# A sheet carried between column strips: four writes cut another way, and one read in place of four

## The chip, the cores and the metric

One core of a Trainium2 chip runs the whole kernel. The metric is the time of one execution in microseconds (us), measured on the device; less is better. The engines are TensorE (PE, with its weight loads PEld apart), VectorE (DVE), ScalarE (ACT), GpSimd (POOL) and SyncE (SP). SP does no arithmetic: it issues DMA transfers, one after another in the order of the program, and stands still where one of them has to wait.

## The reference: what is computed

Two layers of an encoder over 256 tokens of width 2048. Each layer projects the normed input to three groups of heads, works on them, and projects back:

```python
for l in range(DEPTH):                      # DEPTH = 2
    h = rmsnorm(x, norm_g[l])
    proj = h @ w_in[l]                      # 2048 x 7168
    a_x, a_b, a_c, a_g, d_q, d_k, d_v, d_g, m_q, m_g = jnp.split(proj, offsets, axis=-1)
    y_a = short_gated_conv(a_x, a_b, a_c, conv_w[l], conv_b[l]) * jax.nn.silu(a_g)
    # y_d: differential attention, 6 heads, on normed d_q, d_k; gated by silu(d_g)
    # y_m: attention into 256 memory tokens, 4 heads, keys and values from mem @ w_mem_kv[l]
    y = jnp.concatenate([y_a, y_d, y_m], axis=-1) @ w_out[l]
    x = x + y
```

All of it is float32. The two large products, with `w_in` and with `w_out`, are most of the work.

## The kernel before, in words

**The products.** Weights stream from DRAM in tiles of 512 KB (`raw`, 128 partitions x 2 x 512 float32, four buffers; some come as two halves of 256 KB). ACT rounds each to its leading part (`hi`, line 297), DVE makes the rest (`lo`, line 298), and PE multiplies the tokens' two parts (`xT`, `yT`) with them in three passes (line 308): 12 matmuls for a tile. `hi` and `lo` have `PARTS // CK` = 4 buffers each. A few pairs of row tiles go through a scheme with seven products in place of eight (`seven`, line 354; its weights are called `xq` and `wide`). A scheduler sets the order of what isn't pinned; lines with `keep_in_program_order` (often as `pin`) stay as they are written.

**The side work** runs beside the products as generators. `tasks` and `side` hold them, and each `yield n` gives back control for n weight tiles.

**The carry.** The heads need their data with tokens and channels exchanged. DVE's transpose exchanges within blocks of 32 x 32, so what remains is to move blocks: a sheet has 128 partitions = four column strips `a` of 32 partitions, each with four pieces `b` of `r` floats, and piece b of strip a has to go to strip b, as its piece a. `carry(sheet, to)` does that through a DRAM tile `d`, whose order is (b, c, a, r), with c the partition within a strip: four writes (line 492), then `yield 2`, then four reads. All of them are issued by SP and pinned. SP's queue is also that of all weights, so a weight tile that stands behind a read in the program waits until that read is issued, and the read waits until the writes have landed.

Where the target has three dimensions (`len(to.shape) == 3`), strip by strip as it lies in `d`, the reads are those of line 497; where its pieces are laid down in another order (in `pair` and in `turn_sheet(ordered=True)`) they are those of line 499, in runs of 32 floats.

Those who call it: `turn_sheet` (queries and keys `sh`, the memory queries `mqT`, the gates `bgT`), `pair` and `mem_pair` (attention weights `sh`, and the heads' results `yn`), the gate of the memory heads, and `conv` (its input `sh`). In all it is 32 carries of four writes each: 22 with writes of 128 KB, 8 with writes of 64 KB, 2 with writes of 192 KB.

`strips_by_rows` (line 778) is another function and is not changed: POOL issues it to load the first layer's `x` as strips, 32 transfers of 64 KB, `st[:, n] <- src[...].rearrange("p (b r) -> b p r", b=NA)`: 128 partitions in the SBUF, and in DRAM 4 strips of 32 rows of 128 floats.

Of the kernel before, what the change touches and what calls it, by code (L numbers as in the profile page):

```python
# [36 lines left out]
B = 32  # L37
NA = P // B
# [13 lines left out]
def encoder(ctx: ExitStack, tc: tile.TileContext, x, mem, norm_g, w_in, conv_w, conv_b,  # L52
            dq_g, dk_g, lq1, lk1, lq2, lk2, head_g, mem_norm_g, w_mem_kv, mq_g, mk_g, w_out, out):
    nc = tc.nc
# [19 lines left out]
    def nm(s):  # L74
        uid[0] += 1
        return f"{s}_{uid[0]}"
# [391 lines left out]
    def turn_sheet(src, dst=None, of=None, wait=5, ordered=False):  # L468


        if of is None:
            tc.keep_in_program_order(nc.vector.transpose(src, src))
        else:
            for t in range(NT):
                tc.keep_in_program_order(nc.vector.transpose(
                    src[:, :, :, t], of[:, t].rearrange("p (j b c) -> p b j c", b=NA, c=B)))
        flat = src.rearrange("p b j t i -> p b (j t i)")
        if ordered:
            yield wait
            yield from carry(flat, dst.rearrange("p j (t a i) -> p (j t) a i", t=NT, a=NA))  # L480
            return dst
        to = src.rearrange("p b j t i -> p (b j t i)") if dst is None else dst.rearrange("p j r -> p (j r)")
        yield wait
        yield from carry(flat, to.rearrange("p (a r) -> p a r", a=NA))
        return moved(to)

    def carry(sheet, to):


        d = dram.tile([NA, B, NA, sheet.shape[-1]], F32, name=nm("d"))  # L490
        for a in range(NA):
            tc.keep_in_program_order(nc.sync.dma_start(d[:, :, a].rearrange("b c r -> c b r"), sheet[a * B:(a + 1) * B]))
        yield 2
        of = d.rearrange("b c a (n i) -> (b c) a n i", i=B)
        for a in range(NA):
            if len(to.shape) == 3:
                tc.keep_in_program_order(nc.sync.dma_start(to[:, a], d.rearrange("b c a r -> (b c) a r")[:, a]))
            else:
                tc.keep_in_program_order(nc.sync.dma_start(to[:, :, a], of[:, a]))

    def silu2(dst, src, st, t):

# [53 lines left out]
    def pair(heads, begin, end, v):  # L556
# [18 lines left out]
        yield 4  # L575
        flat = sh.rearrange("p b h n c -> p (b h n c)")
        yield from carry(sh.rearrange("p b h n c -> p b (h n c)"), flat.rearrange("p (n a i) -> p n a i", a=NA, i=B))
        eT = flat.rearrange("p (h t k q) -> p h t k q", h=2, t=NT, k=NT)
        while held["yn"] == 2 or held["closed"]:
# [891 lines left out]
```

## Time and profile before

| | us |
|---|---|
| median of 3 runs | 910.44 (910.21 to 910.46) |
| the profiled execution | 910.81 |
| its span in the profile | 909.0 |
| PE busy | 903.3 (99%) |
| DVE busy | 744.6 (82%) |
| ACT busy | 584.5 (64%) |
| DMA queue q1 (SP's), share of the 16 DMA engines' time | 72.1% |

The profile is of one execution. "Busy" is time in which an engine worked on an instruction; the granted TensorE clock is full in all 40 slices of the span. The DMA rows give the transfers by their tiles (`out<-in`), how many there were, the KB of one, and the median time from issue to landing. `SPq` is SP's queue of issues.

### The profile page before, as it was taken

To read this page: it belongs to the slowest core of one execution; us is meant where nothing else is said; L and a number is where in the kernel's file an instruction comes from. 1 tells how busy PE (TensorE), PEld (TensorE's weight loads), DVE (VectorE), ACT (ScalarE), POOL (GpSimd) and SP (SyncE) were. 2 spreads that over 40 slices of the span, in tenths; PEclk is the share of its full clock that TensorE was granted. 3 is DMA by queue.
4 is the path that set the end of the run, shared out by engine and by line. 5 is a ranking of instruction groups with operands and counts; after the bars stand their busy time and mean duration, and the time that the engine had idled before them with its cause. 6 is when DMAs were issued, how large, how long until landed. Compare 5 with 4: busy or idle time off the path is not lost.

```text
span 909.0 us, 12804 instructions
## 1 busy us (share of the span) xinstructions
PE 903.3 (99%) x4161; PEld 744.6 (82%) x4161; DVE 744.6 (82%) x1073; ACT 584.5 (64%) x1135; POOL 135.5 (15%) x197
## 2 busy tenths in 40 slices
PE   9999999999999999999999999999999999999998
PEld 6887888888888888888888888888888888888887
DVE  5558889889888698998799768877987799898896
ACT  6668867757676666655566656676676676655452
POOL 2377241200030101000020202220031101000000
PEclk9999999999999999999999999999999999999999
DMA  8899876678657987879767982878478967988842
GB/s 293 281 260 266 269 269 203 214 255 275 165 187 221 297 247 232 273 251 323 261 197 237 277 276 83 279 255 277 135 235 234 273 219 257 283 272 303 273 157 92
DMA packets 164467, 219.38 MB, mean 241 GB/s; under 512 B 38568, under 2 KB 89576, under 8 KB 164400
## 3 DMA queue, kind: packets, MB, share of 16 engines
q1 hardware_dynamic: 158752, 210.81, 72.1%
q0 software_dynamic: 4448, 6.69, 2.8%
q10 hardware_dynamic: 1200, 1.07, 0.3%
q8 instruction: 32, 0.52, 0.3%
q14 instruction: 35, 0.29, 0.1%
HBM read 197.49 MB, written 21.00 MB: 240 GB/s over the span
## 4 chain that ended last, share of the span: by engine, by line
PE 96%; ACT 2%; DMA 1%; issue 1%; DVE 0%; ACTq 0%
PE acc L308 80%; PE x L354 6%; PE acc L354 5%; PE s L608 1%; PE po L516 1%; DMA raw<-in_w_mem_kv_dram 1%; PE po L745 1%; ACT hi L916 0%; ACT sq L823 0%; PE pt L761 0%; DVE lo L917 0%; ACT xf L795 0%; DMA va<-in_mem_norm_g_dram 0%; PE acc L934 0%; ACT xT L797 0%
## 5 line engine op out<-in xcount | busy, mean ns | idle before, releaser
L308 PE MATMUL acc<-hi,xT 128*128 128x512 f32 x1536 | 482.4, 391 | 0.0
L298 DVE TENSOR_TENSOR lo<-raw,hi 128x1024 fp32r<-128x1024 f32 x238 | 288.3, 1219 | 77.9 <-ACT hi L297 72.7
L297 ACT CAST hi<-raw 128x1024 fp32r<-128x1024 f32 x238 | 248.0, 1050 | 161.9 <-PE acc L308 104.0
L308 PEld LDWEIGHTS acc<-hi,xT 128*128 128x128 f32 x1536 | 288.0, 188 | 60.3 <-ACT hi L297 0.3
L308 PE MATMUL acc<-lo,xT 128*128 128x512 f32 x768 | 299.5, 390 | 0.0
L308 PEld LDWEIGHTS acc<-lo,xT 128*128 128x128 f32 x768 | 144.2, 188 | 29.4
L308 PE MATMUL acc<-hi,yT 128*128 128x512 f32 (+1 forms) x432 | 134.7, 388 | 0.0
L308 PEld LDWEIGHTS acc<-hi,yT 128*128 128x128 f32 x432 | 81.0, 188 | 16.8
L308 PE MATMUL acc<-lo,yT 128*128 128x512 f32 x216 | 83.5, 388 | 0.0
L308 PE MATMUL acc<-hi,memT 128*128 128x512 f32 x248 | 78.6, 393 | 0.0
L381 ACT CAST hi<-xq 128x1024 fp32r<-128x1024 f32 x42 | 44.0, 1049 | 34.7 <-DVE xq L384 19.8
L917 DVE SCALAR_TENSOR_TENSOR lo<-raw,cva,hi 128x1024 fp32r<-128x1024 f32 (+1 forms) x34 | 40.8, 1217 | 22.5 <-ACT hi L916 22.4
L381 DVE TENSOR_TENSOR lo<-xq,hi 128x1024 fp32r<-128x1024 f32 x42 | 51.3, 1222 | 4.7 <-ACT hi L381 4.5
L308 PEld LDWEIGHTS acc<-hi,memT 128*128 128x128 f32 x248 | 46.1, 188 | 9.6 <-ACT hi L916 0.3
L308 PE MATMUL acc<-lo,memT 128*128 128x512 f32 x124 | 48.7, 392 | 0.4 <-DVE lo L917 0.2
L308 PEld LDWEIGHTS acc<-lo,yT 128*128 128x128 f32 x216 | 40.6, 188 | 8.4
L916 ACT ACTIVATE hi<-raw,cva 128x1024 fp32r<-128x1024 f32 (+1 forms) x34 | 36.5, 1098 | 6.9 <-DMA raw<-in_w_mem_kv_dram 6.7
L443 POOL TENSOR_SCALAR ss<-ss,st 128x8 f32<-128x8 f32 (+1 forms) x16 | 12.2, 764 | 179.4 <-ACT sq L440 179.3
L381 ACT CAST hi<-wide 128x1024 fp32r<-128x1024 f32 x21 | 21.8, 1047 | 25.9 <-DVE wide L384 11.3
L354 PE MATMUL x<-hi,yT 128*128 128x512 f32 x96 | 35.4, 390 | 0.0
L192 POOL TENSOR_TENSOR rs<-ss,root 128x8 f32<-128x8 f32 (+1 forms) x20 | 33.4, 1669 | 1.6
L381 DVE TENSOR_TENSOR lo<-wide,hi 128x1024 fp32r<-128x1024 f32 x21 | 25.5, 1221 | 6.1 <-ACT hi L381 6.0
(232 smaller groups left out, 1132.9 us busy)
## 6 DMA issues: line engine op xcount, KB each, us to landing
raw<-in_w_in_dram SPq DMA_DIRECT2D x162, 512.0 KB, 4.7
raw<-in_w_out_dram SPq DMA_DIRECT2D x54, 512.0 KB, 5.1
raw<-in_w_mem_kv_dram SPq DMA_DIRECT2D x30, 512.0 KB, 5.8
raw<-in_w_in_dram SPq DMA_DIRECT2D x60, 256.0 KB, 4.1
xq<-in_w_in_dram SPq DMA_DIRECT2D x52, 256.0 KB, 5.2
d<-sh SPq DMA_DIRECT2D x88, 128.0 KB, 4.5
sh<-d SPq DMA_DIRECT2D x80, 128.0 KB, 4.1
wide<-in_w_out_dram SPq DMA_DIRECT2D x10, 512.0 KB, 6.5
```

Of the source, the lines that this page charges most:

```text
L192: nc.gpsimd.tensor_tensor(r, t, root[:, 0:n], ALU.pow)
L297: nc.scalar.copy(hi, raw)
L298: nc.vector.tensor_tensor(lo_, raw, hi.bitcast(F32), ALU.subtract)
L308: i = nc.tensor.matmul(acc, left, right, start=start, stop=stop)
L354: nc.tensor.matmul(acc, left[a], right[b], start=first and i == 0, stop=last and i == 2)
L381: return ((hi, pin(nc.scalar.copy(hi, src))), (lo, pin(nc.vector.tensor_tensor(lo, src, hi.bitcast(F32), ALU.subtract))))
L443: nc.gpsimd.tensor_scalar(ss[:, t], ss[:, t], 1.0 / gs, col(st, ET, t), ALU.mult, ALU.add)
L516: nc.tensor.matmul(po[:, t, :], eT[:, i, t, k, :], v[:, k, h * P:(h + 1) * P], start=k == 0, stop=k == NT - 1)
L608: pin(nc.tensor.matmul(s[c][:, i, :], yT[rows, a, h, i * P:(i + 1) * P], yT[rows, b, CG + h, :], start=n == 0, stop=n == 2))
L745: nc.tensor.matmul(po, left, right, start=at == 0, stop=at == 3 * NT - 1)
L916: both = (nc.scalar.activation(hi[:, j], raw[:, j], AF.Copy, scale=g), nc.vector.scalar_tensor_tensor(lo[:, j], raw[:, j], g, hi[:, j].bit ...
L917: nc.vector.scalar_tensor_tensor(lo[:, j], raw[:, j], g, hi[:, j].bitcast(F32), ALU.mult, ALU.subtract))
```

## The change

The same four pieces of four strips pass through the same DRAM tile, at the same places in it. What differs is how they are cut into transfers. A write took one strip of 32 partitions with its four pieces, so its two sides were both 32 x 4 x r. Now it takes one piece of all 128 partitions: the SBUF side is 128 x r, and the DRAM side, `d[b].rearrange("c a r -> a c r")`, is 4 x 32 x r. And where the target has three dimensions, one read of 128 partitions x 4r comes in place of four of 128 x r. The reads of line 499 stay.

```diff
         d = dram.tile([NA, B, NA, sheet.shape[-1]], F32, name=nm("d"))
-        for a in range(NA):
-            tc.keep_in_program_order(nc.sync.dma_start(d[:, :, a].rearrange("b c r -> c b r"), sheet[a * B:(a + 1) * B]))
+        for b in range(NA):
+            tc.keep_in_program_order(nc.sync.dma_start(d[b].rearrange("c a r -> a c r"), sheet[:, b]))
         yield 2
+        if len(to.shape) == 3:
+            tc.keep_in_program_order(nc.sync.dma_start(to, d.rearrange("b c a r -> (b c) a r")))
+            return
         of = d.rearrange("b c a (n i) -> (b c) a n i", i=B)
         for a in range(NA):
-            if len(to.shape) == 3:
-                tc.keep_in_program_order(nc.sync.dma_start(to[:, a], d.rearrange("b c a r -> (b c) a r")[:, a]))
-            else:
-                tc.keep_in_program_order(nc.sync.dma_start(to[:, :, a], of[:, a]))
+            tc.keep_in_program_order(nc.sync.dma_start(to[:, :, a], of[:, a]))
```

The order on PE, DVE, ACT and POOL stays as it was; on SP the same transfers stand at the same places, with other shapes. The first place is SP's queue in the first layer, around the memory queries (`mqT`), a pair's attention weights (`sh`) and a pair's results (`yn`), at 279 to 297 us of the profile. The size in a row is that of the side that is written. Before:

```order
L492 DMA d_2978<-sh_2703 32x4x256 x4
L492 DMA d_2983<-sh_2781 32x4x256 x4
L294 DMA raw_2990<-in_w_in_dram 128x2x256 x2
L492 DMA d_3009<-yn_2592 32x4x128 x4
L294 DMA raw_3014<-in_w_in_dram 128x2x256 x2
L497 DMA mqT_2267<-d_2978 128x256 x4
L499 DMA sh_2781<-d_2983 128x8x32 x4
L294 DMA raw_3061<-in_w_in_dram 128x2x256 x2
L497 DMA yn_2592<-d_3009 128x128 x4
```

and with the change:

```order
L492 DMA d_2969<-sh_2694 4x32x256 x4
L492 DMA d_2974<-sh_2772 4x32x256 x4
L294 DMA raw_2981<-in_w_in_dram 128x2x256 x2
L492 DMA d_3000<-yn_2583 4x32x128 x4
L294 DMA raw_3005<-in_w_in_dram 128x2x256 x2
L495 DMA mqT_2258<-d_2969 128x1024
L499 DMA sh_2772<-d_2974 128x8x32 x4
L294 DMA raw_3049<-in_w_in_dram 128x2x256 x2
L495 DMA yn_2583<-d_3000 128x512
```

Nothing changed places: the writes of line 492 have 4 as their outermost count where they had 32, and two groups of four reads are one read each. The second place is SP's queue in the first layer around the gates (`bgT`), a pair's results and a memory pair's attention weights, at 368 to 389 us. Before:

```order
L492 DMA d_3893<-sh_2742 32x4x384 x4
L294 DMA raw_3905<-in_w_in_dram 128x2x512
L294 DMA raw_3925<-in_w_in_dram 128x2x512
L492 DMA d_3943<-yn_3506 32x4x128 x4
L497 DMA bgT_3743<-d_3893 128x384 x4
L294 DMA raw_3960<-in_w_in_dram 128x2x256 x2
L294 DMA raw_3988<-in_w_in_dram 128x2x256 x2
L497 DMA yn_3506<-d_3943 128x128 x4
L492 DMA d_3979<-sh_3794 32x4x256 x4
L294 DMA raw_4024<-in_w_in_dram 128x2x256 x2
L497 DMA sh_3794<-d_3979 128x256 x4
```

and with the change:

```order
L492 DMA d_3869<-sh_2733 4x32x384 x4
L294 DMA raw_3881<-in_w_in_dram 128x2x512
L294 DMA raw_3901<-in_w_in_dram 128x2x512
L492 DMA d_3919<-yn_3488 4x32x128 x4
L495 DMA bgT_3719<-d_3869 128x1536
L294 DMA raw_3933<-in_w_in_dram 128x2x256 x2
L294 DMA raw_3961<-in_w_in_dram 128x2x256 x2
L495 DMA yn_3488<-d_3919 128x512
L492 DMA d_3952<-sh_3770 4x32x256 x4
L294 DMA raw_3994<-in_w_in_dram 128x2x256 x2
L495 DMA sh_3770<-d_3952 128x1024
```

Here too the places are the same; the six weight loads (`raw`) between the first write and the last read have three reads before them or among them where there were twelve.

## The prediction

> **What bounds the kernel now.** First the page's first part and the busy time by stage, the stage being that from the first carry to the last:
>
> ```profile
> PE 903.3 (99%) x4161; PEld 744.6 (82%) x4161; DVE 744.6 (82%) x1073; ACT 584.5 (64%) x1135; POOL 135.5 (15%) x197
> ...
> 150.00:835.00 685.00, 685.00 (x3195) 567.11 (x3194) 578.43 (x857) 447.11 (x887) 73.46 (x104) 1.00 0.77 244
> ```
>
> The second row's columns are the stage, its length, then busy us and count of PE, PEld, DVE, ACT and POOL, the granted clock, the DMA share and GB/s. PE is busy in 685.00 of 685.00 us. TensorE is the bound, and in the stage of the carries there is no wait of it that a faster carry could shorten. So the change can win next to nothing; the question is whether it costs. Then the DMA side, the queue of SP and the carries' transfers:
>
> ```profile
> q1 hardware_dynamic: 158752, 210.81, 72.1%
> ...
> d<-sh SPq DMA_DIRECT2D x88, 128.0 KB, 4.5
> sh<-d SPq DMA_DIRECT2D x80, 128.0 KB, 4.1
> ```
>
> The first row gives packets, MB and the share of 16 DMA engines' time. It gives the rate of one DMA engine while it works: 210.81 MB / (0.721 x 16 x 909.0 us) = 20.1 bytes per ns. A write of 128 KB needs 131072 / 20.1 = 6.52 us of one engine's time: 0.41 us if 16 share it. Of its 4.5 us to landing the rest is latency and what stands ahead of it. Last, who waits in SP's queue:
>
> ```profile
> SPq L497 <- DMA d<-sh: 15.1, 16, 2.8
> ...
> 368.34 2.99 SPq L492 DMA_DIRECT2D d<-sh  x4
> 371.82 1.06 SPq L294 DMA_DIRECT2D raw<-in_w_in_dram  x2
> 372.98 2.06 SPq L492 DMA_DIRECT2D d<-yn  x4
> 375.28 3.64 SPq L497 DMA_DIRECT2D bgT<-d  x4
> 379.02 2.18 SPq L294 DMA_DIRECT2D raw<-in_w_in_dram  x4
> ```
>
> In 16 places the read already waits for the writes to land (15.1 us in all, 2.8 at most), and weights (`raw`) are queued right behind it. Whatever makes a write land later holds up weights.
>
> **Step 1: over how many DMA engines a write is spread.** All writes of before have 32 as the outermost count of both sides. Those of after have 128 in the SBUF and 4 in DRAM. No SP transfer of before has such sides, but POOL's loads of `x` (line 778) do, the other way round: 4 x 32 rows in DRAM, 128 partitions in the SBUF. Their stage, 46 to 82 us:
>
> ```profile
> DMA packets 4413, 8.92 MB, mean 248 GB/s; under 512 B 2127, under 2 KB 2127, under 8 KB 4409
> ...
> raw<-in_w_mem_kv_dram SPq DMA_DIRECT2D x11, 512.0 KB, 5.8
> xt<-in_x_dram POOLq DMA_DIRECT2D x32, 64.0 KB, 5.7
> xq<-in_x_dram SPq DMA_DIRECT2D x1, 512.0 KB, 8.6
> kd<-sh POOLq DMA_DIRECT2D x3, 128.0 KB, 4.8
> ```
>
> 64 KB with these sides take 5.7 us, 128 KB of the same queue with the old sides (`kd<-sh`, 32 x 4 x 256) 4.8. And the small packets: all rows of these transfers are 512 B or longer, so a packet under 512 B carries no data. Suppose that each transfer leaves one on each of 16 engines: 47 transfers make 752, but there are 2127. The 1375 too many are 43 for each `xt` load. That is near 48 = 12 x 4, as if 12 of 16 engines had only empty pieces to do, four each, and 4 engines carried all. It is an inference, but I take from it that such a transfer runs on four DMA engines, and SP's writes as well. The ends are a cost of 0 (16 engines, as every SP transfer has now) and that of four.
>
> [...]
>
> On four engines a write of 128 KB takes 6.52 / 4 = 1.63 us of each in place of 0.41. A carry of four such writes puts 4 x 1.22 = 4.9 us more on each of the four; of 64 KB 2.4 us, of 192 KB 7.3 us. In all 22 x 4.9 + 8 x 2.4 + 2 x 7.3 = 142 us. Every weight tile needs all 16 engines, so it lands when the last of the four is done.
>
> **Step 2: what of it the four engines have room for.** DMA share by stage, cut around the carries; columns as above:
>
> ```profile
> 278.00:307.00 29.00, 29.00 (x150) 24.02 (x149) 21.13 (x42) 19.78 (x40) 0.83 (x4) 1.00 0.87 250
> 307.00:340.00 33.00, 33.00 (x156) 27.57 (x155) 27.29 (x42) 21.91 (x46) 3.58 (x6) 1.00 0.90 275
> 344.00:357.00 13.00, 13.00 (x67) 11.02 (x66) 12.23 (x21) 8.35 (x20) 2.18 (x3) 1.00 0.81 252
> 366.00:396.00 30.00, 30.00 (x139) 24.94 (x139) 27.35 (x40) 18.02 (x26) 0.00 (x0) 1.00 0.93 295
> 404.00:428.00 24.00, 24.00 (x113) 20.09 (x112) 19.43 (x31) 11.82 (x17) 0.00 (x0) 1.00 0.95 320
> 686.00:714.00 28.00, 28.00 (x143) 22.87 (x142) 18.96 (x39) 17.54 (x41) 4.19 (x10) 1.00 0.92 264
> 714.00:745.00 31.00, 31.00 (x148) 25.88 (x147) 26.57 (x42) 20.79 (x43) 1.21 (x3) 1.00 0.88 271
> 749.00:763.00 14.00, 14.00 (x74) 11.93 (x74) 13.86 (x23) 9.88 (x22) 1.63 (x3) 1.00 0.91 293
> 771.00:801.00 30.00, 30.00 (x140) 24.94 (x140) 26.90 (x40) 17.66 (x26) 0.00 (x0) 1.00 0.92 292
> 808.00:834.00 26.00, 26.00 (x122) 21.74 (x121) 23.31 (x40) 13.67 (x19) 0.00 (x0) 1.00 0.95 315
> 150.00:206.00 56.00, 56.00 (x247) 45.98 (x246) 49.98 (x59) 37.94 (x96) 9.42 (x8) 1.00 0.76 255
> 230.00:245.00 15.00, 15.00 (x68) 12.35 (x67) 12.68 (x14) 8.43 (x11) 0.00 (x0) 1.00 0.80 210
> 576.00:626.00 50.00, 50.00 (x233) 41.31 (x233) 35.21 (x39) 33.27 (x87) 10.45 (x8) 1.00 0.87 285
> 652.00:668.00 16.00, 16.00 (x84) 12.43 (x83) 13.58 (x24) 9.41 (x24) 3.82 (x4) 1.00 0.84 239
> ```
>
> An engine's room in a stage is (1 - share) x length. The first stage has two carries of 128 KB writes and one of 64 KB, 12.2 us more on each of the four; room 0.13 x 29 = 3.8; late by 8.4. In the same way, in the order of the rows: 12.2 - 3.3 = 8.9; 4.9 - 2.5 = 2.4; 14.7 - 2.1 = 12.6; 7.3 - 1.2 = 6.1; then the second layer's 12.2 - 2.2 = 10.0; 12.2 - 3.7 = 8.5; 4.9 - 1.3 = 3.6; 14.7 - 2.4 = 12.3; 7.3 - 1.3 = 6.0; and the four looser stages 14.7 - 13.4 = 1.3; 4.9 - 3.0 = 1.9; 14.7 - 6.5 = 8.2; 4.9 - 2.6 = 2.3. All together 92.5 us late.
>
> **Step 3: what the weights' lead hides.**
>
> ```profile
> 16.35 5.48 PE acc L308 x24
> ...
> L298 DVE TENSOR_TENSOR lo<-raw,hi 128x1024 fp32r<-128x1024 f32 x238 | 288.3, 1219 | 77.9 <-ACT hi L297 72.7
> L297 ACT CAST hi<-raw 128x1024 fp32r<-128x1024 f32 x238 | 248.0, 1050 | 161.9 <-PE acc L308 104.0
> ...
> 394.72 1.05 ACT L297 CAST hi<-raw 128x1024 fp32r<-128x1024 f32 x1 [1.85 <-DMA raw<-in_w_in_dram]
> ```
>
> 24 matmuls take 5.48 us, so a weight tile (12) feeds PE for 2.74 us. Of four `hi`/`lo` buffers one is being read, the other three hold 8.2 us; less ACT's and DVE's own 1.05 + 1.22 us for one tile, 5.9 us. That is the lead if no `raw` tile waits ready. The last row shows ACT, in the stage 366 to 396, waiting 1.85 us for a tile to land: there no `raw` tile is ready. Elsewhere ACT mostly waits for PE to give back a buffer (104.0 us), so landed tiles do lie ready; all four would be 11.0 us more, a lead of 16.9. I take 5.9, because the crowded stages are those with a row that shows the empty end.
>
> A stage that follows the one before without a gap finds no lead rebuilt (307 to 340, 714 to 745). The sum: 2.5 + 8.9 + 0 + 6.7 + 0.2 in the first layer, 4.1 + 8.5 + 0 + 6.4 + 0.1 in the second, 2.3 in 576 to 626, else 0: 39.7 us.
>
> Lower end: a lead of 16.9 leaves 0.4 of the pair 8.4 + 8.9 and 1.6 of 10.0 + 8.5: 2 us. Upper end: no lead, 92.5 us.
>
> **Step 4: the rest.** The one read moves the same bytes. Three issues fewer in 26 carries, but four writes that may each take longer to issue:
>
> ```profile
> L492 SPq DMA_DIRECT2D d<-sh x104: 302/436/1237, 154.2 to 824.9; - x104
> L497 SPq DMA_DIRECT2D sh<-d x64: 319/432/1359, 160.7 to 829.4; - x64
> L778 POOL DMA_DIRECT2D xt<-in_x_dram x32: 677/677/785, 46.3 to 79.5; - x32
> ```
>
> Three reads at 432 ns save 1.3 us of SP a carry. Writes at POOL's 677 ns for such sides, the far end, cost 4 x 0.24 = 1.0 us. I put both at nothing: within a carry they nearly cancel, and the covering work is SP's own wait for the writes. DVE and ACT get the sheet some 5 us later; in-order work behind them is late by as much, and it comes out of the same lead, which is already spent in the sum. That pushes up, not down.
>
> **The sum.** 910.81 + 39.7 = 950.5 against the profiled execution; the median of the runs is 0.4 us under that execution: 950.
>
> **The rivals.**
>
> *The writes spread over 16 engines after all* (the four-engine reading holds for POOL's queue alone). For it: all SP transfers of before do. Then bytes, rows and places are the same and PE stays the bound: 910, within 0.2%, which is about what a measurement here can tell from no change.
>
> *Four engines, but the lead is deep.* For it: ACT's 104.0 us of waits for PE. Against it: the row at 394.72. 912 to 925.
>
> *Four engines and hardly any lead*, with DVE's lateness on top. Over 985, up to 910.8 + 92.5 = 1003.
>
> *Faster*, one mechanism: the write of before takes its bytes from 32 partitions; from 128 it could land sooner, and the read behind it, for which SP waits 15.1 us now, is issued sooner. Price: 128 KB into 128 partitions (`sh<-d`) land in 4.1 us, out of 32 in 4.5, so up to 0.4 us a write. It decides from the point where PE waits for a carry; the stage row, 685.00 of 685.00, says that it never does by more than the rows can show. Its time is 907 at best, if half of 16 x 0.4 us reached PE.
>
> [...]
>
> **Chances.** Four engines with the lead of step 3, 925 to 985: 0.62. Deep lead: 0.14. Hardly any lead: 0.10. Sixteen engines: 0.09. Faster: 0.05. So slower 0.86, the same 0.09, faster 0.05. The likeliest gives 950. The range 913 to 985 leaves out sixteen engines, faster, and the worse part of hardly any lead, some 0.2.
>
> **What would show it.** Step 1: `d<-sh` of 128 KB lands in 8 us or more where it took 4.5, and the DMA share of SP's queue stays near 72% of a longer span while GB/s falls in the carries' stages. Step 2: SP's wait of the read for the writes goes from 15.1 us to some 100 us. Step 3: PE's idle time, 5.7 us now, rises to about 45, in the stages 278 to 340, 366 to 396 and their like in the second layer, ended by `hi` or `lo`, and ACT's waits for `raw` rise with it. The prediction is wrong if the writes land in 4 to 5 us as now, or if PE stays at 99% although they land late.

## The result and the profile after

| | before | after |
|---|---|---|
| median, us | 910.33 (909.87 to 910.46, 4 runs) | 959.42 (958.20 to 961.91, 4 runs) |
| ratio | | 1.0541 (95% interval 1.0521 to 1.0560) |
| the profiled execution, us | 910.81 | 961.91 |
| its span, us | 909.0 | 960.0 |
| PE busy, us | 903.3 | 925.3 |
| PE idle (span less busy), us | 5.7 | 34.7 |

The change costs 49 us, 51 between the two profiled executions: PE stands 29.0 us longer and is busy 22.0 us longer for the same 4161 matmuls. First the page's first part, the DMA packets and SP's queue, of the kernel after:

```profile
PE 925.3 (96%) x4161; PEld 748.8 (78%) x4161; DVE 741.4 (77%) x1073; ACT 582.5 (61%) x1135; POOL 133.8 (14%) x197
...
DMA packets 151697, 219.35 MB, mean 228 GB/s; under 512 B 35784, under 2 KB 73480, under 8 KB 151632
...
q1 hardware_dynamic: 145984, 210.80, 67.0%
```

and the row of packets of the kernel before:

```profile
DMA packets 164467, 219.38 MB, mean 241 GB/s; under 512 B 38568, under 2 KB 89576, under 8 KB 164400
```

The small packets can be read as a count of engines. In the trace of before, SP's 690 transfers left 11040 packets of 4 B on its queue, 16 for each, and the page counts 16 DMA engines: one on each. After the change there are 38568 - 35784 = 2784 fewer. The change takes away 26 x 3 = 78 reads; at 16 small packets each these are 1248. The 1536 that are left are 128 x 12: each of the 128 writes has 12 small packets fewer, four in place of 16, so by this reading it runs on four engines. The count comes out to the last packet.

The semaphores, the counters by which a transfer tells that it has landed, say the same. In the trace of before, the landing of a transfer raises its semaphore in 16 steps: 12288 steps for 768 transfers. The kernel after has 9632 steps for 690 transfers, which is 16 for each of the 562 others and 5 for each of the 128 writes (8992 + 640). Of a write's five, the first comes a median of 1.0 us after the start of its issue, the other four some 5 us later. The page gives no time to landing for SP's transfers of the kernel after; counted off in these steps, a 128 KB write lands a median of 7.2 us after the start of its issue (3.4 to 9.7), where it was 4.5.

The chain of work that ended last, before `PE 96%`, by engine and by line:

```profile
PE 53%; DMA 16%; DVE 14%; ACT 6%; issue 5%; SPq 5%; POOL 1%; ACTq 0%; DVEq 0%
PE acc L308 43%; DMA raw<-in_w_in_dram 7%; DVE lo L298 4%; DMA d<-sh 4%; PE x L354 4%; PE acc L354 3%; ACT hi L297 3%; SPq L492 3%; DMA raw<-in_w_out_dram 3%; DMA xq<-in_w_in_dram 1%; DVE lo L381 1%; SPq L294 1%; DVE xq L384 1%; ACT hi L381 1%; DVE xq L1133 1%
```

PE's share falls to 53%. In its place stand, among others, weights on their way (`raw`, 7% and 3%), the writes on their way (`d<-sh`, 4%), and SP issuing the writes (`SPq L492`, 3%). The waits of the queue and the engines that go with them (us in total, times, longest):

```profile
SPq L495 <- DMA d<-sh: 52.7, 25, 4.5
...
SPq L499 <- DMA d<-sh: 13.9, 6, 3.3
...
SPq L495 <- DMA d<-yn: 8.1, 6, 2.4
...
ACT hi L297 <- DMA raw<-in_w_in_dram: 101.1, 37, 6.7
ACT hi L297 <- DMA raw<-in_w_out_dram: 32.9, 13, 7.1
...
PE acc L308 <- ACT hi L297: 11.8, 11, 1.9
PE acc L308 <- DVE lo L298: 8.1, 13, 0.8
```

Before, the casts' waits were these:

```profile
ACT hi L297 <- DMA raw<-in_w_in_dram: 19.4, 12, 2.7
ACT hi L297 <- DMA raw<-in_w_out_dram: 2.0, 1, 2.0
```

SP waits at the reads for 74.7 us. ACT's casts (line 297) wait 134.0 us for weights in 50 places, where it was 21.4 us in 13, and PE waits for `hi` and `lo`. The issues of line 492 (min/median/max in ns):

```profile
L492 SPq DMA_DIRECT2D d<-sh x104: 503/552/2229, 154.2 to 875.4; - x104
L492 SPq DMA_DIRECT2D d<-yn x24: 508/1237/3316, 289.3 to 827.3; - x24
```

The shortest issue went from 302 to 503 ns, the longest from 1237 to 3316. Summed over all 128 writes, SP spends 109.5 us on issuing them, where it was 56.8.

**What it looks like at one place.** SP's queue at the first pair of carries, before:

```profile
279.26 4.16 SPq L492 DMA_DIRECT2D d<-sh  x8
283.52 1.11 SPq L294 DMA_DIRECT2D raw<-in_w_in_dram  x2
284.68 2.11 SPq L492 DMA_DIRECT2D d<-yn  x4
286.88 0.91 SPq L294 DMA_DIRECT2D raw<-in_w_in_dram  x2
```

and after, with two casts that wait for their weights at the end:

```profile
279.18 7.79 SPq L492 DMA_DIRECT2D d<-sh  x8
287.08 2.19 SPq L294 DMA_DIRECT2D raw<-in_w_in_dram  x2
289.32 5.13 SPq L492 DMA_DIRECT2D d<-yn  x4
294.55 1.51 SPq L294 DMA_DIRECT2D raw<-in_w_in_dram  x2
...
295.66 1.05 ACT L297 CAST hi<-raw 128x1024 fp32r<-128x1024 f32 x1 [3.44 <-DMA raw<-in_w_in_dram]
300.29 1.05 ACT L297 CAST hi<-raw 128x1024 fp32r<-128x1024 f32 x1 [2.27 <-DMA raw<-in_w_in_dram]
```

Both start at 279.2. The weights that went out at 286.88 go out at 294.55, 7.7 us later, and the profile shows no wait of SP for a semaphore in between: all of it is issuing (7.79 + 5.13 against 4.16 + 2.11 us for the twelve writes, and 1.1 us more on the weights between them). The chain goes the same way. It follows SP through the twelve writes and the weights among them up to 295.59, then it has this row:

```profile
295.59 4.35 DMA raw<-in_w_in_dram
```

These weights land in 4.35 us, about as before, so the chain puts the delay down to SP. But the four engines show here too. The two halves of a weight tile that SP issued right behind the eight writes, at 287.08, took 7.8 and 7.3 us to land (from the semaphores), where the same two took 3.9 and 4.2 before, and the cast at 295.66 waited 3.44 us for them.

SP's issues themselves lengthen as writes pile up: of the eight, the first five took 0.5 to 0.8 us each, the last three 1.3 to 1.5. Over the run an issue of a write takes a median of 0.52 us with at most one earlier write still on its way, and 1.4 us with four or more (50 and 27 writes). Before, these were 0.43 and 0.45 (50 and 20). So part of SP's longer issuing looks like a wait for the same four engines. What SP does within an issue, no run shows.

At later places the chain holds these rows:

```profile
403.75 6.54 DMA raw<-in_w_in_dram
...
425.71 8.25 DMA d<-sh
...
435.00 6.78 DMA raw<-in_w_out_dram
...
448.81 7.61 DMA raw<-in_w_out_dram
```

This write takes 8.25 us to land, and the weights 6.5 to 7.6. Over the run, a weight tile of 512 KB that is issued while a carry's writes are on their way takes a median of 7.8 us to land (36 tiles), where it was 5.7 (34); the others take 4.8, where it was 4.7. Where a cast waited for weights, it started a median of 5.9 us after their issue; before it was 4.7 (50 and 13 such casts in the traces).

**Where the loss accrues.** PE's matmuls are the same in both kernels and in the same order, so the start of the n-th can be compared; by how much it is later after the change is called its lag. By the time of before, with the terms of the prediction beside them:

| stage, us | growth of the lag, us | predicted, us |
|---|---|---|
| to 278 | -0.1 | 0 |
| 278 to 354 | 8.9 | 11.4 |
| 354 to 415 | 5.9 | 6.7 |
| 415 to 454 | 6.5 | 0.2 |
| 454 to 633 | 0.0 | 2.3 |
| 633 to 685 | 6.6 | 0 |
| 685 to 754 | 11.7 | 12.6 |
| 754 to 834 | 5.9 | 6.4 |
| 834 to the end | 5.7 | 0.1 |
| sum | 51.1 | 39.7 |

The windows of busy time in parts of those stages, of the kernel after (columns as in the prediction):

```profile
278.00:312.00 34.00, 31.03 (x150) 24.72 (x149) 18.23 (x38) 17.81 (x35) 0.83 (x4) 0.97 0.65 195
312.00:349.00 37.00, 36.44 (x163) 29.10 (x162) 28.43 (x44) 22.59 (x48) 3.97 (x6) 0.98 0.73 234
376.00:411.00 35.00, 33.40 (x154) 27.11 (x152) 26.70 (x37) 17.16 (x26) 0.00 (x0) 1.00 0.61 202
```

The DMA side is less busy than before, not more: 0.87 became 0.65, 0.93 became 0.61, and 250 and 295 GB/s became 195 and 202. That fits twelve engines that have little to do while four, or SP, are the limit; the profile doesn't list the engines one by one.

### The profile page after: what moved, and what is told of

Same layout as the page of the kernel before. It is cut to its first block, busy times and chain, and to the rows that moved or that the text cites. A ratio compares the mean times of both kernels' runs of the same rounds, so it can differ in the third digit from the quotient of the medians.

```text
span 960.0 us, 12665 instructions
## 1 busy us (share of the span) xinstructions
PE 925.3 (96%) x4161; PEld 748.8 (78%) x4161; DVE 741.4 (77%) x1073; ACT 582.5 (61%) x1135; POOL 133.8 (14%) x197
## 2 busy tenths in 40 slices
DMA packets 151697, 219.35 MB, mean 228 GB/s; under 512 B 35784, under 2 KB 73480, under 8 KB 151632
## 4 chain that ended last, share of the span: by engine, by line
PE 53%; DMA 16%; DVE 14%; ACT 6%; issue 5%; SPq 5%; POOL 1%; ACTq 0%; DVEq 0%
PE acc L308 43%; DMA raw<-in_w_in_dram 7%; DVE lo L298 4%; DMA d<-sh 4%; PE x L354 4%; PE acc L354 3%; ACT hi L297 3%; SPq L492 3%; DMA raw<-in_w_out_dram 3%; DMA xq<-in_w_in_dram 1%; DVE lo L381 1%; SPq L294 1%; DVE xq L384 1%; ACT hi L381 1%; DVE xq L1133 1%
## 5 line engine op out<-in xcount | busy, mean ns | idle before, releaser
L308 PE MATMUL acc<-hi,xT 128*128 128x512 f32 x1536 | 488.9, 395 | 8.6 <-ACT hi L297 8.6
L308 PE MATMUL acc<-lo,xT 128*128 128x512 f32 x768 | 304.1, 396 | 6.4 <-DVE lo L298 6.4
L308 PEld LDWEIGHTS acc<-lo,xT 128*128 128x128 f32 x768 | 146.0, 190 | 41.2 <-DVE lo L298 11.4
L308 PE MATMUL acc<-hi,yT 128*128 128x512 f32 (+1 forms) x432 | 136.7, 390 | 5.2 <-ACT hi L297 3.2
L381 ACT CAST hi<-wide 128x1024 fp32r<-128x1024 f32 x21 | 21.8, 1047 | 27.5 <-DVE wide L384 11.8
L192 POOL TENSOR_TENSOR rs<-ss,root 128x8 f32<-128x8 f32 (+1 forms) x20 | 32.4, 1618 | 1.6
```

What stands on the lines that cost most here:

```text
L192: nc.gpsimd.tensor_tensor(r, t, root[:, 0:n], ALU.pow)
L308: i = nc.tensor.matmul(acc, left, right, start=start, stop=stop)
L381: return ((hi, pin(nc.scalar.copy(hi, src))), (lo, pin(nc.vector.tensor_tensor(lo, src, hi.bitcast(F32), ALU.subtract))))
```

## The experiments

The theory going in (F, in the expectations): the writes run on four of 16 DMA engines, and what needs all 16 comes late. The rivals: the read is what costs (R), or SP's time in issuing and standing (S).

**One part at a time.** The old writes with the one read:

```diff
-        for b in range(NA):
-            ... dma_start(d[b].rearrange("c a r -> a c r"), sheet[:, b])
+        for a in range(NA):
+            ... dma_start(d[:, :, a].rearrange("b c r -> c b r"), sheet[a * B:(a + 1) * B])
```

> The old writes (one strip of 32 partitions each) with the new single read of 128 x 4r. Theory F (the new writes run on four DMA engines, whose lateness holds up the weights): 908 to 912, as the kernel before, since the writes are spread over 16 engines again. Rival R (the change costs through its read: one transfer of up to 768 KB in a burst pushes the weights behind it): 930 to 960. Rival S (the new writes keep SP longer, 109.5 us of issuing in place of 56.8, and this is what delays the weights): 908 to 912 too.

910.57 us, ratio 1.0002 (0.9992 to 1.0011). It has 37320 packets under 512 B: its 78 reads fewer account for the 1248, 16 each, by themselves. And the new writes with the old four reads, the opposite edit:

> The new writes (all 128 partitions, 4 x 32 x r in DRAM) with the old four reads. F: 958 to 970, the whole loss and some more, since three more issues of SP come behind each late write. R: 908 to 915. S: 958 to 970.

964.34 us, ratio 1.0591 (1.0560 to 1.0621). So all of the loss is in the writes. The read alone changes nothing that can be measured while PE is the bound.

**The cut or the engines.** In 26 of the 32 carries (104 writes) all 128 partitions are written at once, but into a DRAM tile that keeps the partitions' order, so that both sides are 128 x r. The reads pick the strips out again. The other six carries stay as they were.

```diff
-        d = dram.tile([NA, B, NA, sheet.shape[-1]], F32, name=nm("d"))
+        d = dram.tile([NA, P, r], F32, name=nm("d"))
+        for b in range(NA):
+            ... dma_start(d[b], sheet[:, b])
+        yield 2
+        for b in range(NA):
+            ... dma_start(to[b * B:(b + 1) * B], d[b].rearrange("(a c) r -> c a r", a=NA))
```

> The 26 carries with a target of three dimensions write pieces of all 128 partitions, but into a DRAM tile in the order (b, a, c, r), where the 128 rows of a write lie flat, 128 x r on both sides; four reads of 32 partitions take them back; the other 6 carries as before. F: 128 rows on both sides spread over 16 engines, so 908 to 914 although each write takes all partitions. If writing from all 128 partitions at once were what costs: 940 to 960. S: 908 to 914 if SP needs about 0.43 us for such a write.

911.48 us, ratio 1.0015 (1.0003 to 1.0028). The next kernel differs from that one only in a gap of 64 floats after each 32 rows in DRAM, which makes the DRAM side 4 x 32 x r:

```diff
-        d = dram.tile([NA, P, r], F32, name=nm("d"))
+        d = dram.tile([NA, 4, 32 * r + 64], F32, name=nm("d"))
```

> The same as with flat rows, but 64 floats are left free in the DRAM tile after each 32 rows, so that a write's DRAM side is 4 x 32 x r; bytes, partitions, number of transfers and reads are those of the flat one. F: this form runs on four engines, so 26 of 32 carries pay again: 940 to 955, and in the count of small packets 104 x 12 = 1248 fewer than with flat rows. If the shape didn't set the engines: as flat. S: 940 to 955 if SP needs longer for the form.

966.87 us, ratio 1.0632 (1.0602 to 1.0662): more than either theory had said, and about as much as the new writes with four reads. The kernel without the gap has the packets of the kernel before, 38568 of them under 512 B. With the gap:

```profile
DMA packets 163219, 219.37 MB, mean 228 GB/s; under 512 B 37320, under 2 KB 88328, under 8 KB 163152
```

1248 small packets fewer, 104 x 12, and 5 steps of the semaphore for each of the 104 writes where there are 16 without the gap. The same bytes from the same partitions in the same order cost 1 us with 128 as the outermost count of both sides, and 56 us where one side has 4. What decides is the shape of the DRAM side, and with it the number of engines. A gap after each 64 rows instead gives 2 x 64 x r, two engines (with eight half reads a carry):

> As the flat tile with gaps, but the gap stands after each 64 rows, so that a write's DRAM side is 2 x 64 x r; the reads come in two halves of 32 partitions each (8 in place of 4). F: such a write runs on two engines, 6.52 / 2 = 3.26 us for 128 KB where four need 1.63, so the four writes of a carry put 11.4 us more on each of the two engines than 16 would, against 4.9 on each of the four: a loss of 2 to 2.5 times the 56 us that the gaps after 32 rows cost, 1020 to 1055; packets under 512 B fall by 104 x 2 against four engines, but rise by 104 x 16 for the added reads. S: SP's issues of 208 reads more than with four reads (no, 104 more) cost some 45 us and the writes' form is as before: 970 to 1010.

1090.14 us, ratio 1.1969 (1.1951 to 1.1986), above both ranges. Its packets:

```profile
DMA packets 164676, 219.39 MB, mean 201 GB/s; under 512 B 38776, under 2 KB 89784, under 8 KB 164608
```

By the count: 104 reads more add 104 x 16 = 1664, writes on 14 engines fewer take off 104 x 14 = 1456; 38568 + 208 = 38776. So 16, 4 and 2 engines cost 1, 56 and 179 us. Half as many engines as four more than triple the loss, of which the half reads, 42 us more of SP's issuing, are a part that was not run apart. Landing and issuing grow together: with 16, 4 and 2 engines a 128 KB write of this form lands a median of 4.4, 6.2 and 9.8 us after the start of its issue, and SP needs 56.2, 90.0 and 193.3 us to issue the 128 writes.

**SP's time without the four engines.** Each write cut into four of 32 partitions: 16 short writes a carry, and the one read. By the small packets (43464 in all, 16 for each write) they run on 16 engines.

```diff
         for b in range(NA):
-            ... dma_start(d[b].rearrange("c a r -> a c r"), sheet[:, b])
+            for a in range(NA):
+                ... dma_start(d[b, :, a], sheet[a * B:(a + 1) * B, b])
```

> Each of the four writes is cut into four, one strip's piece of 32 partitions x r, so that both sides have 32 rows and 16 engines share them; one read, as in the changed kernel. SP has 512 writes to issue in place of 128, at about 0.43 us some 220 us in place of 56.8 before and 109.5 in the changed kernel. S (SP's time is what delays the weights): over 1000, since SP loses three times what the changed kernel loses. F: 910 to 925, each write on 16 engines; a little for SP, since the last write of a carry is issued 5 us later.

1006.69 us, ratio 1.1057 (1.1041 to 1.1074). F expected 910 to 925 and misses by over 80 us; S expected over 1000. The issues of its writes of sheets, and its waits of SP and ACT:

```profile
L493 SPq DMA_DIRECT2D d<-sh x416: 302/419/2027, 155.1 to 919.6; - x139
```

```profile
SPq L493 <- DMA raw<-in_w_in_dram: 29.5, 33, 3.2
...
ACT hi L297 <- DMA raw<-in_w_in_dram: 116.7, 49, 10.2
ACT hi L297 <- DMA raw<-in_w_out_dram: 41.0, 17, 9.2
```

One issue is as short as before (302 ns at least), but there are 512: 215.8 us in all against 60.3 for the old writes with one read. The casts wait for weights longer than with the change, though a waiting cast starts 4.9 us after the issue of its weights, about as before. So the waiting casts' weights land about as fast as ever and are issued too late. SP also stands 29.5 us at these writes until earlier weights have landed. SP's time, in issuing and standing, is a way to lose a tenth though every write runs on 16 engines; the two parts of it were not run apart.

**The wait at the read.** The changed kernel with the read two weight tiles later:

```diff
-        yield 2
+        yield 4
```

> The changed kernel with the read two weight tiles later behind the writes (yield 4 in place of 2), so that the weights don't stand behind a read that waits. If the loss comes of SP standing still at the read until the late writes land (74.7 us of such waits in the changed kernel): 915 to 930. If it comes of the four engines themselves being behind, so that each weight tile lands late wherever the read stands: 945 to 962.

934.00 us, ratio 1.0253 (1.0238 to 1.0269), between the two ranges. The same edit to the kernel before, as a control:

> The control of the run with the later read: the kernel before with its reads two weight tiles later. No theory expects more than 908 to 915.

921.69 us, ratio 1.0115 (1.0096 to 1.0134), a miss: a carry that comes back two tiles later costs 11 us by itself. The waits with the change and the later read:

```profile
SPq L495 <- DMA d<-sh: 25.0, 21, 2.3
...
ACT hi L297 <- DMA raw<-in_w_in_dram: 75.6, 35, 6.9
```

The later read takes 25 us off the changed kernel. Against its own control the change costs 934.0 - 921.7 = 12 us, where it costs 49 with the read at its place. SP's issuing is nearly as long as with the change (101.2 us for the writes, against 109.5; control 58.1), and the writes are the same. So half of the loss hangs on the read coming before the writes have landed, with SP standing at it, and three quarters of it if the control's 11 us simply add to it, which is not shown.

**Another queue.** POOL issues all of the carry, and the old carry the same way as its control:

```diff
-    ... nc.sync.dma_start(d[b] ...), nc.sync.dma_start(to ...)
+    ... nc.gpsimd.dma_start(d[b] ...), nc.gpsimd.dma_start(to ...)
```

> The changed kernel with every carry's writes and reads issued by POOL instead of SP; the cut, and so the four engines, stays. Theory Q (the weights are late because SP, which issues them in order, stands: 52.7 us longer in issuing the writes, 56 us longer in waits at the reads): both are gone from SP, so most of the 51 us goes: 908 to 922. Theory L (the four engines' queues delay the part of each weights' transfer that they carry, whoever issues the writes): 940 to 962. In the experiments so far, where a cast waited for weights, issue to use was 6.0 us in the changed kernel against 4.7 us before, and 4.9 us in the version of sixteen writes: that speaks for L's share being the smaller one, about a third.

964.18 us, ratio 1.0575 (1.0528 to 1.0622).

> Control: the kernel before with its carries' writes and reads issued by POOL. Both theories: 905 to 916, if POOL's issuing is not itself waited for; what it comes to above 910.5 is the price of the other queue and is to be taken off the version with the changed cut.

933.92 us, ratio 1.0252 (1.0236 to 1.0267). Both miss: POOL's queue costs the old carry 23 us, and with the change it is 30 us more. With those 23 us taken off, as the control was meant for, the changed carry stands at 941 us: at the low edge of what L expected, and far above Q. The DMA issues of the control (the old cut), with the median time to landing at the end:

```profile
d<-sh POOLq DMA_DIRECT2D x88, 128.0 KB, 3.7
...
d<-sh POOLq DMA_DIRECT2D x8, 192.0 KB, 6.2
```

and of the version with the changed writes, with its waits:

```profile
d<-sh POOLq DMA_DIRECT2D x88, 128.0 KB, 6.4
...
d<-sh POOLq DMA_DIRECT2D x8, 192.0 KB, 9.4
```

```profile
POOL sh L495 <- DMA d<-sh: 82.1, 13, 9.4
...
ACT hi L297 <- DMA raw<-in_w_in_dram: 22.1, 13, 3.2
...
ACT hi L297 <- DMA raw<-in_w_out_dram: 13.3, 9, 3.9
...
PE po L516 <- DMA sh<-d: 6.7, 1, 6.7
```

On this queue too a write of the new cut lands later: 6.4 us in place of 3.7. The casts wait 35.4 us for weights, not 134.0. But now PE stands for the sheet itself (`po` waits 6.7 us at one place for the read of `sh`), 15.7 us of the lag accrue in the heads' work at 715 to 754, and 14.1 do in the control. The place of the wait moved, and the sum did not fall. With only the reads, or only the writes, on POOL:

> The changed kernel with only the reads issued by POOL: SP no longer stands at the read, and has 42 us less to issue, but still takes 109 us to issue the writes. Theory Q: of the 109 us that SP lost, 56 and the reads' issue are gone; 915 to 933. Theory L: 940 to 962, as the engines are as uneven as before.

950.12 us, ratio 1.0428 (1.0403 to 1.0453).

> The changed kernel with only the writes issued by POOL: SP's long issuing is gone, its wait at the read stays (or grows, if POOL takes longer to put the writes out). Theory Q: 920 to 942. Theory L: 945 to 965.

962.94 us, ratio 1.0588 (1.0553 to 1.0622). Both lie in L's ranges and above Q's. The casts' waits with the reads on POOL:

```profile
ACT hi L297 <- DMA raw<-in_w_in_dram: 82.9, 28, 6.9
...
ACT hi L297 <- DMA raw<-in_w_out_dram: 25.7, 15, 5.7
```

and with the writes on POOL:

```profile
ACT hi L297 <- DMA raw<-in_w_in_dram: 22.7, 14, 5.1
...
ACT hi L297 <- DMA raw<-in_w_out_dram: 6.4, 4, 2.7
```

Moving the reads leaves 108.6 us of the 134.0; moving the writes leaves 29.1. The lag that accrues between 278 and 454 us of before, a stage full of carries, puts the versions side by side:

| kernel | lag, 278 to 454 us |
|---|---|
| the change | 21.3 |
| sixteen writes on 16 engines | 43.5 |
| two engines | 70.6 |
| the change, read two tiles later (control) | 10.0 (5.5) |
| the change, all on POOL (control) | 13.5 (2.2) |
| the change, reads on POOL | 12.9 |
| the change, writes on POOL | 9.7 |

The later read and each move to POOL remove 8 to 12 of the 21 us, and none removes all. These lags are less sharp than that of the change: in the versions with 16 writes, the later read or POOL, 354 to 895 of PE's 4161 matmuls come at another place in its order. In the POOL versions PE also stands for late sheets, which gives SP time to catch up, so their smaller waits for weights can't be put down to SP alone. **What stays open** is how the 49 us divide between the longer issuing, the wait at the reads and the slower landing. All three are seen on the chain, the issues lengthen while landings are slow, and no run with the new cut takes one of them away and leaves the others as they were. None of the versions is faster than the kernel before. No run here shows which engine carried what, on SP's queue or on POOL's.

## Why the prediction was right, point by point

*950.0 against 959.42 us, slower as forecast, inside the range.* The mechanism, few engines, was the right one. The sum was 9 us short of the median, and that it came so near is in part luck, as its misses go both ways: the stages that it took for crowded cost 4.7 us less than it gave them, and three that it took for harmless cost 18.5 us more.

*Step 1, four engines.* Right, and shown for SP's queue, as far as the counts can show it: the packets and the semaphores' steps of the change, of the gap in DRAM and of two engines all come out to the last one. A write with 4 x 32 x r in DRAM leaves 4 small packets and takes 5 steps, one with 128 x r on both sides 16 and 16, one with 2 x 64 x r 2 and 3. For a weight tile, which by the step needs all 16, the steps are 16 in both kernels. The step had inferred the four engines from POOL's loads, though the sign that it read there, too many small packets (43 a load), is the opposite of SP's, which has fewer; and POOL's loads raise their semaphore in 16 steps, as all transfers of before do, so their four engines were not shown. The sign foretold for it was half right. The writes do land later, but the median of the 128 KB ones is 7.2 us, not 8 or more, and on POOL's queue 6.4, 2.7 us more than with the old cut. And the share of q1 did not stay near 72%: it is 67.0% of 960.0 us, 643 us of each engine against 655 before. A longer span with the same bytes has to lower it. GB/s fell in the carries' stages, as said.

*Step 2, lateness from the engines' room, 92.5 us.* Right that SP's wait at the reads would rise, 18.7 (15.1 + 3.2 + 0.4) to 74.7 us (some 100 were foretold). But the step took the lateness to be the four engines' backlog, which every weight tile has to wait out. Weights issued while such writes are on their way do land later, 7.8 us in place of 5.7. The waiting casts' weights took a median of 5.9 us in place of 4.7, 1.2 us more, while the waits of the casts average 134.0 / 50 = 2.7 us. The rest is best explained by weights that SP issued late.

*Step 3, a lead of 5.9 us.* The total is near: PE idles 29.0 us more, against 39.7, and is waiting for `hi` and `lo`. In the stages to which the step gave more than 6 us, it gave 37.1 us and 32.4 were measured. It failed at three places to which it gave 0.3 us together and which cost 18.8: 415 to 454, 633 to 685 and the end. The step took the lead to be whole at the start of each such stage, from rooms alone. At 633 to 650 little was left of it. A weight tile issued right behind four writes took 8.85 us to land, on the chain of waits, and the cast waited 6.74 us for it:

```profile
640.55 8.85 DMA raw<-in_w_in_dram
```

```profile
649.49 1.05 ACT L297 CAST hi<-raw 128x1024 fp32r<-128x1024 f32 x1 [6.74 <-DMA raw<-in_w_in_dram]
```

That is the backlog of step 2 itself, in a place where the room and the lead were counted on to hide it.

*Step 4, SP's issuing "at nothing".* This is the step that failed. It gave at most 1.0 us a carry, thought the reads' saving of 1.3 about as large, and said that SP's own wait covers it. Issuing the writes costs 52.7 us more over the run, 1.6 a carry, and issuing the weights (`raw`) 21.6 more (150.8 in place of 129.2); the reads save 27.5 (41.8 in place of 69.3). So the parts don't cancel. At 279 to 295 us no wait of SP is seen that could cover them, and the 7.7 us by which the weights go out later are SP's issuing. POOL's issue times could not show this: there a carry's write of the new cut never took more than 773 ns to issue, while SP's issues lengthen with the writes on their way (from 0.52 to 1.4 us). The sixteen writes show what SP's time can cost, 96 us, with its standing at the writes. The read's saving was real but without worth: the old writes with one read run in 910.57 us.

*A term that was not in the sum: the clock.* The windows of one stretch and of the time ahead of it, of the kernel after, the granted clock being the third number from the end:

```profile
306.70:310.10 3.40, 1.56 (x6) 1.07 (x7) 1.84 (x3) 2.67 (x5) 0.00 (x0) 1.00 1.01 343
...
310.10:313.50 3.40, 3.40 (x10) 2.66 (x9) 2.42 (x3) 2.58 (x4) 0.00 (x0) 0.50 0.83 275
```

Five times (310.1, 412.5, 665.1, 777.7 and 849.4 us) the clock is half for 3.4 us, each time after 3.4 us in which PE was busy for 1.3 to 1.9. By an estimate, half of 3.4 us lost each time, that is 5 x 1.7 = 8.5 us, most of the gap between the 39.7 and the 51.1 us; it is part of the 22.0 us by which PE is busy longer. What makes up the rest of those is not shown, nor what sets the clock to half: in the window ahead PE was not idle, only busy less than six tenths of it (1.93 of 3.40 us at most).

*The rivals.* Sixteen engines on SP's queue: excluded by the packets. Faster from 128 partitions at once: on 16 engines they gave 911.48 us, no gain, as the bound is PE (busy 903.3 of 909.0 us before). Deep lead, 912 to 925: excluded, the time is 34 us above it. Hardly any lead, over 985 us: not on four engines; the time is 26 us below it.

## What to carry to other kernels

Count over how many DMA engines a transfer runs before cutting it another way: by the packets here, a DRAM side whose outermost count is 4 put it on four of 16 (49 us), and an order in DRAM with 128 outermost on both sides made the same cut all but free (1 us). Price a transfer on the queue that issues it, too, by issue time and not by bytes alone, when weights stand behind it in the same queue; sixteen short writes cost 96 us here, twice the 49 of the four bad ones. And where PE has no idle time to give back, a short stall can cost more than its length: here five stretches of 3.4 us, with PE busy for 1.3 to 1.9, were each followed by 3.4 us at a granted clock of 0.50.

## What was not expected of the hardware

- SP took longer to issue a write that, by its packets, ran on fewer engines: 302 ns at least on 16, 503 on four, and up to 3316 ns for the last of eight writes at 380 to 393 us, with the two halves of a weight tile among them. On POOL's queue the same change took 691 ns in place of 552, and never over 773.
- SP's writes that left 4 small packets raised their semaphore in 5 steps, those that left 2 in 3, those that left 16 in 16. So in these traces the number of engines could be counted a second way, and with it the landing, where the page prints none. POOL's loads of `x` took 16 steps like all the rest.
- SP's transfers left 16 packets of 4 B each before (11040 for 690), and after the change 4 for each write and 16 for each of the others (8256 = 128 x 4 + 484 x 16). The sixteen writes fit too: 384 writes more and 78 reads fewer make 38568 + 6144 - 1248 = 43464, and 43464 were counted. On POOL's queue it is not so: with all of the changed carry there the kernel has 23784 of them, its control 13992, though it has 78 reads fewer.
- A granted clock of 0.50 came, five times, after stretches in which PE was still busy for 1.3 to 1.9 of 3.4 us.
- A carry that comes back two weight tiles later costs the old kernel 11 us, and one through POOL's queue 23, though SP is relieved in both.
